# A hybrid encoder layer: weighing spread over two tiles, banks emptied during a pass's last tile, sparse sums added by VectorE, one normalization for both token tiles

## The chip, the cores and the metric

The kernel runs on one core of a Trainium2 chip. The metric is the device time of one execution in microseconds (us). TensorE (PE) multiplies, VectorE (DVE) and ScalarE (ACT) work on elements, GpSimd (POOL) issues the indirect DMAs, and SyncE (SP) issues the loads of weights. ACT issues DMAs too; each engine takes its instructions, DMAs among them, in order.

## The reference

One layer over 272 tokens of width 2048 (16 learned ones in front, 256 of the input): two mixers, a projection and a normalization, then a product-key expert layer, a second normalization, and the 256 input tokens as output. Only the expert layer and what follows matter here:

```python
qh = (xb @ w_pq).reshape(P_BLOCK, P_HEADS, 2, P_QDIM // 2)
...
eidx = jnp.take_along_axis(cidx, pos, axis=-1).reshape(P_BLOCK, P_HEADS * P_TOPK)
g = jax.nn.softmax(top, axis=-1).reshape(P_BLOCK, P_HEADS * P_TOPK).astype(xb.dtype)
act = jax.nn.gelu(jnp.einsum('td,tkd->tk', xb, u_tab[eidx]))
return jnp.einsum('tk,tkd->td', g * act, v_tab[eidx])
...
h = layer_norm(ALPHA * h + peer_ffn(h, w_pq[l], sub_keys[l], u_tab[l], v_tab[l]), ln2_g[l], ln2_b[l])
```

Each token picks 128 of 16384 experts; u_tab and v_tab are 16384 x 2048 each.

## The kernel before

For 224 of the 256 tokens (NT) the expert layer is computed densely: all activations gelu(x . u) for all experts, times a mostly zero matrix of weights g, times v. For the other 32 tokens (NS) it is computed sparsely, from gathered rows.

**u pass.** Tile j holds 128 experts; it comes as two half tiles of 128 x 1024 (n counts half tiles). `begin` loads one more half tile (SP, `raw`, 4 buffers) and splits it into two parts: ACT casts it to `wh` (L134), DVE subtracts to get `wl` (L137), 4 buffers each. In steady work the split of a unit is issued three units ahead of its matmuls. `product` issues a wl matmul (L1114) and a wh matmul over both halves of the input (L1115), three matmuls at the head of a bank (L1110 to L1112). `activation` empties the bank of a tile (`gather_out`: ACT copies the low half, L1055, DVE adds, L1057) and ACT applies the Gelu: for tiles below HELD = 70 into `slots` in SBUF, for later ones into spill groups of four (`ya`, in the same three buffers as `wv`, L1073), which ACT stores to `ad` in DRAM (L1075).

**The weights g.** POOL scatters them, 256 indirect DMAs (L957), into `gd` in DRAM. The sparse tokens' rows come by 32 indirect loads of u_rows and 32 of v_tab (L1031), two buffers; DVE uses each (L1018 for u, L1025 for v). `sparse(rate)` spreads these: 0.33 credits twice a tile in u from tile 28 on, 0.14 twice a tile in the value passes; each whole credit issues one fetch or one use.

**Value passes.** v is taken in two passes h = 0, 1 of 128 tiles, each tile 128 experts x 1024 columns, 8 column blocks d; bank `pv[d]` sums over the 128 tiles. The moving operand is made by `weigh(i)` for a pair of tiles: DVE multiplies the activations by the weights (L1094; in pass 1 only for the tiles that are loaded again, the others keep their product), ACT copies to `wv` (L1097), DVE subtracts (L1099). In even tiles its steps are issued after d = 0, 3 and 6, for the pair two further on. At the end of it ACT issues the next loads: weights (L1085), and for tiles from `far` = 108 on activations into one of two `ring` buffers (L1087). Tiles 70 to 107 come back in five bulk loads into `late[0]` (tile `over`, L1228). Pairs 0 and 1 are weighed at the last two half tiles of u.

**Between the passes** all eight banks are emptied after the last tile into `tmp` and stored to `fd` by ACT (L1247). **At the end** the last tile's banks are emptied behind each d, `turn_back(c, t)` turns 512 columns of a token tile t back with TensorE (L1262; for t = 1 also a `comb` matmul that adds the four parts of the sparse sums, L1261), DVE adds the residual (L1264) and takes statistics (L217); `ln2_finish(t)` normalizes each token tile by itself with DVE (L1279, L1283, L1285), ACT (L1276, L1281) and POOL (L1277, L1284).

PE, DVE, ACT and SP keep the order in which the program issues instructions; POOL's order is set by the scheduler.

Of the kernel before, what the change touches and what calls it, by code (L numbers as in the profile page):

```python
# [40 lines left out]
HELD, LATE = 70, 38  # L41
# [6 lines left out]
def hybrid_layer(ctx: ExitStack, tc: tile.TileContext, a: dict):  # L48
# [824 lines left out]
    gts = [home(2 * NT).rearrange("p (j t) -> p j t", t=NT) for _ in range(2)]  # L873
# [6 lines left out]
    ring = [mem[:, picks + 2 * NT * i:picks + 2 * NT * (i + 1)].rearrange("p (j t) -> p j t", t=NT) for i in range(2)]  # L880
# [199 lines left out]
    def fetch_weights(i):  # L1080

        h, m = divmod(i, P // 2)
        j = 2 * m
# [132 lines left out]
    later.append((P + 80, comb, a["c_comb"]))  # L1216
    for t in range(2):
        later.append((P + 81 + 2 * t, res[:, 4 * t:4 * t + 4, :NT], fd[4 * t:4 * t + 4].rearrange("d p t -> p d t")))
    for i in range(2):
        later.append((P + 88 + 8 * i, row2[i], a["ln_rows"][4 + i:5 + i, :].broadcast_to([P, D])))  # L1220
    stage = None
    for h in range(2):
        pv = [psum() for _ in range(8)]
        for j in range(P):
# [28 lines left out]
    st2 = [sm.tile([P, 4, 6], F32, name="bnst") for _ in range(2)]

    def turn_back(c, t):
        cs = slice(c * 512, (c + 1) * 512)
        ps = psum()
        for q in range(4):
            if t:

                nc.tensor.matmul(ps[:, q * P:(q + 1) * P], comb[:U], xsp[:U, c * 512 + q * P:c * 512 + (q + 1) * P], start=True, stop=False)  # L1261
            nc.tensor.matmul(ps[:, q * P:(q + 1) * P], res[:, 4 * c + q, t * P:(t + 1) * P], ident, start=t == 0, stop=True)  # L1262
        dst = fin[:, t, cs]
        nc.vector.scalar_tensor_tensor(out=dst, in0=dst, scalar=ALPHA, in1=ps, op0=ALU.mult, op1=ALU.add)  # L1264
# [111 lines left out]
```

## Time and profile before

| | |
|---|---|
| median of 3 runs | 1963.23 us (1961.41 to 1966.65) |
| the profiled execution | 1960.09 us, span 1958.3 us |
| busy: PE, weight load, DVE, ACT, POOL | 96%, 90%, 72%, 50%, 34% of the span |
| mean granted TensorE clock | 0.982 |
| u pass, about | 590 to 1239 us |
| value passes, about | 1243 to 1589 and 1591 to 1931 us |

A busy time is the sum over an engine's instructions; a granted clock of 1.00 is 2.4 GHz, 0.50 is 1.2 GHz. "idle before <- X" is the time for which the engine had nothing to do ahead of that instruction, and what ended it.

### The profile page before, as it was taken

The page shows a single profiled execution, that of the slowest core. Times are in us where ns is not written, and L with a number is a line of the kernel's source. Part 1 is how long each engine was busy: PE and PEld are TensorE (multiplying, and loading weights), DVE is VectorE, ACT ScalarE, POOL GpSimd, SP SyncE. Part 2 cuts the span into 40 slices and gives each one's busy share as a digit, 9 for nine tenths or more (in the row PEclk, how much of TensorE's full clock was granted, in tenths as well). Part 3 has the DMA queues.
Part 4 walks back from the last instruction along what each step waited for, and adds up shares of the span by engine and source line. Part 5 has one row for each costly group of instructions (what it writes and reads, how often), then busy time and mean ns, then how long its engine had stood idle before and what let it go on. Part 6 is the DMA issues. An engine that isn't in the chain of part 4 may idle for free.

```text
span 1958.3 us, 32249 instructions
## 1 busy us (share of the span) xinstructions
PE 1873.9 (96%) x12376; PEld 1761.0 (90%) x12376; DVE 1418.1 (72%) x2163; ACT 977.0 (50%) x1458; POOL 668.2 (34%) x381
## 2 busy tenths in 40 slices
PE   7999999998999999999999999899999879999995
PEld 5998998887999999899999999899999879999995
DVE  7674586656878999976767667677887667776767
ACT  5553554534446565455555545444554445555542
POOL 4000004001388883787877877010001011110002
PEclk9999998999999999999999999899999989999998
DMA  6974444364667787899999999799888867779882
GB/s 209 329 269 166 169 146 146 132 216 159 204 174 203 196 247 229 253 277 297 288 290 293 309 296 321 273 338 334 308 316 307 299 233 273 264 259 327 295 266 74
DMA packets 183293, 488.80 MB, mean 250 GB/s; under 512 B 52553, under 2 KB 83537, under 8 KB 173137
## 3 DMA queue, kind: packets, MB, share of 16 engines
q1 hardware_dynamic: 115312, 371.61, 55.6%
q0 software_dynamic: 47712, 76.41, 15.0%
q10 hardware_dynamic: 20112, 38.71, 5.5%
q8 instruction: 97, 1.59, 0.3%
q14 instruction: 60, 0.48, 0.1%
HBM read 458.92 MB, written 26.59 MB: 248 GB/s over the span
## 4 chain that ended last, share of the span: by engine, by line
PE 49%; DVE 10%; DMA 6%; issue 4%; ACT 4%; ACTq 0%; POOL 0%; DVEq 0%
PE ps L1115 29%; PE ps L1114 15%; DVE wl L137 4%; DMA raw<-v_tab 3%; ACT wh L134 2%; DMA raw<-u_tab 2%; PE ps L181 1%; PE ps L180 1%; PE ps L179 1%; DVE mem L1025 1%; DVE mem L1094 1%; DVE wv L1099 1%; PE ps L1112 1%; PE ps L1111 1%; ACT wv L1097 1%
## 5 line engine op out<-in xcount | busy, mean ns | idle before, releaser
L137 DVE TENSOR_TENSOR wl<-raw,wh 128x1024 fp32r<-128x1024 f32 x660 | 804.0, 1230 | 393.5 <-ACT wh L134 372.0
L134 ACT CAST wh<-raw 128x1024 fp32r<-128x1024 f32 x666 | 692.5, 1049 | 668.4 <-PE ps L1115 204.9
L1115 PE MATMUL ps<-wv,wh 128*128 128x448 f32 x2032 | 643.2, 376 | 0.0
L1115 PE MATMUL ps<-actT,wh 128*128 128x448 f32 x1920 | 603.7, 370 | 0.0
L1114 PE MATMUL ps<-wv,wl 128*128 128x224 f32 x2032 | 541.9, 267 | 12.2 <-DVE wl L137 12.1
L1114 PE MATMUL ps<-actT,wl 128*128 128x224 f32 x1920 | 511.1, 266 | 5.3 <-DVE wl L137 4.4
L957 POOL DMA_INDIRECT gd<-mem x256 | 486.9, 1902 | 83.4 <-issue 74.7
L1115 PEld LDWEIGHTS ps<-wv,wh 128*128 128x128 f32 x2032 | 383.9, 189 | 29.0
L1114 PEld LDWEIGHTS ps<-wv,wl 128*128 128x128 f32 x2032 | 390.5, 192 | 18.0 <-DVE wl L137 17.9
L1115 PEld LDWEIGHTS ps<-actT,wh 128*128 128x128 f32 x1920 | 359.8, 187 | 20.9
L1114 PEld LDWEIGHTS ps<-actT,wl 128*128 128x128 f32 x1920 | 365.4, 190 | 7.8 <-DVE wl L137 6.7
L179 PE MATMUL ps<-actT,wh 128*128 128x256 f32 (+1 forms) x944 | 277.4, 294 | 4.9 <-ACT actT L350 4.9
L180 PE MATMUL ps<-actT,wh 128*128 128x256 f32 (+1 forms) x944 | 271.9, 288 | 4.4 <-POOL actT L229 4.2
L181 PE MATMUL ps<-actT,wl 128*128 128x256 f32 (+1 forms) x944 | 270.7, 287 | 0.0
L1031 POOL DMA_INDIRECT mem<-v_tab,mem x32 | 56.0, 1749 | 532.2 <-DVE mem L1025 477.2
L179 PEld LDWEIGHTS ps<-actT,wh 128*128 128x128 f32 x944 | 181.4, 192 | 12.6 <-ACT actT L350 5.1
L180 PEld LDWEIGHTS ps<-actT,wh 128*128 128x128 f32 x944 | 181.4, 192 | 7.1 <-POOL actT L229 5.8
L181 PEld LDWEIGHTS ps<-actT,wl 128*128 128x128 f32 x944 | 181.1, 192 | 0.0
L1097 ACT CAST wv<-mem 128x448 fp32r<-128x448 f32 x90 | 50.8, 564 | 123.7 <-DVE mem L1094 121.1
L1099 DVE TENSOR_TENSOR wv<-mem,wv 128x448 fp32r<-128x448 f32 x90 | 56.1, 623 | 31.0 <-ACT wv L1097 31.0
L1031 POOL DMA_INDIRECT mem<-u_rows,mem x32 | 50.5, 1577 | 71.0 <-DVE mem L1018 57.6
L1018 DVE CUSTOM_DVE_ANT_0 mem<-mem 128x2048 f32<-128x2048 f32 x32 | 73.1, 2285 | 0.0
(281 smaller groups left out, 1652.5 us busy)
## 6 DMA issues: line engine op xcount, KB each, us to landing
raw<-u_tab SPq DMA_DIRECT2D x256, 512.0 KB
raw<-v_tab SPq DMA_DIRECT2D x256, 512.0 KB
raw<-w_in SPq DMA_DIRECT2D x86, 512.0 KB
mem<-gd ACTq DMA_DIRECT2D x74, 224.0 KB
raw<-w_out SPq DMA_DIRECT2D x32, 512.0 KB
raw<-w_pq SPq DMA_DIRECT2D x32, 512.0 KB
gd<-mem SPq DMA_DIRECT2D x16, 896.0 KB
ad<-ya ACTq DMA_DIRECT2D x14, 448.0 KB
```

The lines of the kernel that those rows point to most:

```text
L134: acts.append(order(nc.scalar.copy(out=wh, in_=raw)))
L137: subs.append(order(nc.vector.tensor_tensor(out=wl, in0=raw, in1=wh.bitcast(F32), op=ALU.subtract)))
L179: nc.tensor.matmul(out, wh, ah, start=first, stop=False)
L180: nc.tensor.matmul(out, wh, al, start=False, stop=False)
L181: nc.tensor.matmul(out, wl, ah, start=False, stop=last)
L957: s = nc.gpsimd.indirect_dma_start(out=gdf[:, :], out_offset=bass.IndirectOffsetOnAxis(ap=idx, axis=0), in_=val, in_offset=None, compute_o ...
L1018: nc.vector.tensor_tensor_reduce(out=buf[:U], in0=buf[:U], in1=xsp[:U], scale=1.0, scalar=0.0, op0=ALU.mult, op1=ALU.add, accum_out=sact[: ...
L1031: f = nc.gpsimd.indirect_dma_start(out=buf[:U], out_offset=None, in_=a["u_rows" if n < K else "v_tab"], in_offset=bass.IndirectOffsetOnAxi ...
L1097: nc.scalar.copy(out=w[:, :, 0], in_=x)
L1099: nc.vector.tensor_tensor(out=w[:, :, 1], in0=x, in1=w[:, :, 0].bitcast(F32), op=ALU.subtract)
L1114: nc.tensor.matmul(lo, wl, x[:, 0], start=False, stop=False)
L1115: nc.tensor.matmul(two(ps)[:, :, :NT], wh, x, start=False, stop=last)
```

## The change

`weigh` becomes four steps: the mult after d = 0 of an even tile; copy and load of weights after d = 0 of the odd one; the subtraction after its d = 5; the load of activations after d = 3 of the next even tile. Loads run three pairs ahead, in three buffers each, and HELD falls from 70 to 68 to make room. The first three weight loads stand 12 half tiles before the end of u instead of 2, pair 0 is weighed 4 half tiles before the end, pair 1 after the last activation. The sparse rate in u is 0.34, and 0 in the last two tiles. The banks of pass 0 are emptied behind each d of its last tile, into other buffers (`spare`), with no sparse step there. The sparse sums are added in pass 1: POOL copies three 32-row parts of `xsp` to `over` at tile 110, and DVE adds the four parts into `fin` at tiles 114, 116, 118 and 120. `ln2_finish` runs once: one chain for both tiles, ACT scales tile 1, DVE does the rest, and POOL nothing.

```diff
-HELD, LATE = 70, 38
+HELD, LATE = 68, 38
...
-        if i < P and (h == 0 or j >= far):
-            nc.scalar.dma_start(out=gts[m % 2], in_=gd[:, j:j + 2])
+        if i < P and (h == 0 or 2 * m >= far):
+            nc.scalar.dma_start(out=gts[i % 3], in_=gd[:, 2 * m:2 * m + 2])
+    def fetch_activations(i):
+        j = 2 * (i % (P // 2))
         if i < P and j >= far:
-            nc.scalar.dma_start(out=ring[m % 2], in_=ad[:, j - HELD:j - HELD + 2])
+            nc.scalar.dma_start(out=ring[i % 3], in_=ad[:, j - HELD:j - HELD + 2])
...
         if h == 0 or j >= far:
-            nc.vector.tensor_tensor(out=x, in0=x, in1=gts[m % 2], op=ALU.mult)
-            yield
+            nc.vector.tensor_tensor(out=x, in0=x, in1=gts[i % 3], op=ALU.mult)
+        yield
         w = g.tile([P, 2, 2, NT], F32R, name="wv", bufs=3)
         nc.scalar.copy(out=w[:, :, 0], in_=x)
+        fetch_weights(i + 3)
         yield
         nc.vector.tensor_tensor(out=w[:, :, 1], in0=x, in1=w[:, :, 0].bitcast(F32), op=ALU.subtract)
         wv[i] = w
-        fetch_weights(i + 2)
+        yield
+        fetch_activations(i + 3)
...
-        if n == 2 * P - 2:
+        if n == 2 * P - 12:
             scatter_some(len(scatters))
-            fetch_weights(0)
-            fetch_weights(1)
+            for m in range(3):
+                fetch_weights(m)
...
-                    sparse(0.33 if j >= 28 else 0)
+                    sparse(0.34 if 28 <= j < P - 2 else 0)
...
-        if n == 2 * P - 2:
+        if n == 2 * P - 4:
             whole_of(weigh(0))
-        if n == 2 * P - 1:
-            whole_of(weigh(1))
...
     whole_of(activation(P - 1, ps))
+    whole_of(weigh(1))
...
+            if h == 1 and j == 110:
...
+                for i in range(G - 1):
+                    nc.gpsimd.dma_start(out=others[i][ND:], in_=xsp[i * NS:(i + 1) * NS])
+            if h == 1 and j >= 114 and j % 2 == 0 and joined[0] < G:
...
+                    nc.vector.scalar_tensor_tensor(out=own, in0=own, scalar=ALPHA, in1=xsp[ND:], op0=ALU.mult, op1=ALU.add)
...
+                    nc.vector.tensor_tensor(out=own, in0=own, in1=others[i - 1][ND:], op=ALU.add)
...
-                if j % 2 == 0 and d in (0, 3, 6) and stage:
-                    next(stage, None)
-                if d == 4:
+                if d == 0 or (d == 5 and j % 2):
+                    next(now, None)
+                if d == 3 and j % 2 == 0 and before:
+                    next(before, None)
+                if d == 4 and not (h == 0 and j == P - 1):
                     sparse(0.14)
-        if h == 0:
-            for d in range(8):
-                y = tmp()[:, :NT]
-                whole_of(gather_out(two(pv[d]), y))
-                nc.scalar.dma_start(out=fd[d], in_=y)
+                if h == 0 and j == P - 1:
+                    y = spare(d)
+                    whole_of(gather_out(two(pv[d]), y))
+                    nc.scalar.dma_start(out=fd[d], in_=y)
...
+    def ln2_finish():
+        nm = sm.tile([P, 2], F32, name="nb")
+        rsqrt_eps(mv2[:, 1], mv2[:, 1], 1.0)
...
+            nc.scalar.activation(out=fin[:, 1, cs], in_=fin[:, 1, cs], func=AF.Identity, scale=mv2[:, 1, 1:2], bias=nm[:, 1:2])
...
+            nc.vector.scalar_tensor_tensor(out=y, in0=y, scalar=mv2[:, 0, 0:1], in1=row2[0][:, cs], op0=ALU.subtract, op1=ALU.mult)
+            nc.vector.scalar_tensor_tensor(out=y, in0=y, scalar=mv2[:, 1, 0:1], in1=row2[1][:, cs], op0=ALU.mult, op1=ALU.add)
...
+            nc.vector.tensor_tensor(out=y, in0=y, in1=row2[0][:, cs], op=ALU.mult)
+            nc.vector.tensor_tensor(out=y, in0=y, in1=row2[1][:, cs], op=ALU.add)
```

The order that this makes is seen at three places. First DVE near the end of pass 0, before (`mem<-mem` and `over` of 128x448 are the mult, `wv` the subtraction, L1025 a sparse row):

```order
L1099 TENSOR_TENSOR wv<-mem,wv 128x2x224
L137 TENSOR_TENSOR wl<-raw,wh 128x1024 x2
L1094 TENSOR_TENSOR mem<-mem 128x448
L1025 SCALAR_TENSOR_TENSOR mem<-mem 128x2048
L1099 TENSOR_TENSOR wv<-mem,wv 128x2x224
```

and changed:

```order
L1104 TENSOR_TENSOR wv<-mem,wv 128x2x224
L137 TENSOR_TENSOR wl<-raw,wh 128x1024
L1098 TENSOR_TENSOR mem<-mem 128x448
L1025 SCALAR_TENSOR_TENSOR mem<-mem 128x2048
L137 TENSOR_TENSOR wl<-raw,wh 128x1024
L1104 TENSOR_TENSOR wv<-mem,wv 128x2x224
```

A wl, for which DVE waits for a cast of ACT and not for the copy, now stands between the mult and the subtraction of a pair. Second ACT from the first load of weights to the copy of pair 2, before:

```order
L1085 DMA mem<-gd 128x448 x2
L1055 COPY tmp<-ps 128x224
L1073 ACTIVATE ya<-tmp 128x224
L1075 DMA ad<-ya 128x896
L1097 CAST wv<-mem 128x2x224
L1085 DMA mem<-gd 128x448
L134 CAST wh<-raw 128x1024
L1097 CAST wv<-mem 128x2x224
L1085 DMA mem<-gd 128x448
L1073 ACTIVATE ya<-tmp 128x224
L1055 COPY tmp<-ps 128x224
L1073 ACTIVATE ya<-tmp 128x224
```

and changed, from the copy of pair 0 on:

```order
L1101 CAST wv<-mem 128x2x224
L1084 DMA mem<-gd 128x448
L134 CAST wh<-raw 128x1024 x2
L1055 COPY tmp<-ps 128x224
L1073 ACTIVATE ya<-tmp 128x224
L134 CAST wh<-raw 128x1024
L1073 ACTIVATE ya<-tmp 128x224
L1055 COPY tmp<-ps 128x224
L1073 ACTIVATE ya<-tmp 128x224
L1075 DMA ad<-ya 128x896
L1101 CAST wv<-mem 128x2x224
L1084 DMA mem<-gd 128x448
```

The copies of pairs 0 and 1 no longer stand ahead of the last two Gelus; pair 0's comes ahead of three casts, pair 1's behind the last store. Third DVE in pass 1 about tile 116, changed (L1250 and L1252 are the sparse additions; before there is no such instruction):

```order
L1250 SCALAR_TENSOR_TENSOR mem<-mem 32x2048
L1098 TENSOR_TENSOR mem<-mem 128x448
L137 TENSOR_TENSOR wl<-raw,wh 128x1024
L1104 TENSOR_TENSOR wv<-mem,wv 128x2x224
L137 TENSOR_TENSOR wl<-raw,wh 128x1024
L1252 TENSOR_TENSOR mem<-mem,over 32x2048
```

One addition stands in front of the mult of each of four pairs.

## Rows read from the trace of the kernel before

**Rows 1.** Busy time by stretch: start:end, length, PE, PEld, DVE, ACT, POOL, PEclk, DMA share, GB/s

```profile
1239.45:1255.09 15.64, 8.69 (x39) 7.81 (x39) 7.91 (x11) 6.24 (x12) 0.37 (x1) 0.67 0.72 248
1255.09:1588.70 333.61, 322.50 (x2019) 303.13 (x2017) 259.57 (x269) 159.51 (x191) 30.74 (x18) 0.99 0.88 312
1588.70:1606.64 17.94, 10.45 (x37) 8.42 (x37) 7.44 (x13) 4.88 (x10) 2.38 (x1) 0.62 0.59 202
1606.64:1922.57 315.93, 314.79 (x2006) 299.70 (x2005) 217.87 (x209) 157.20 (x184) 20.68 (x13) 1.00 0.78 272
1922.57:1958.30 35.73, 13.82 (x113) 13.22 (x111) 28.83 (x56) 8.23 (x16) 9.89 (x6) 0.76 0.16 60
```

**Rows 2.** Timeline, u to v: start, duration, engine, line, out<-in, [idle before <- releaser]

```profile
1240.39 0.33 ACTq L1075 DMA_DIRECT2D ad<-ya  x1
...
1242.64 0.37 PE L1110 MATMUL ps<-wv,wh 128*128 128x224 f32 x1 [3.04 <-ACT wv L1097]
...
1249.16 0.39 ACT L1073 ACTIVATE ya<-tmp 128x224 f32<-128x224 f32 x1 [3.23 <-DMA ad<-ya]
...
1255.09 0.26 PE L1114 MATMUL ps<-wv,wl 128*128 128x224 f32 x1
```

**Rows 3.** Waits of PE in 1255.09 to 1588.7: total us, times, longest

```profile
PE ps L1114 <- DVE wl L137: 10.9, 12, 1.9
```

**Rows 4.** Timeline of DVE and ACT at the end of pass 0

```profile
1525.15 0.62 DVE L1094 TENSOR_TENSOR mem<-mem 128x448 f32<-128x448 f32 x1
...
1525.80 0.57 ACT L1097 CAST wv<-mem 128x448 fp32r<-128x448 f32 x1 [4.01 <-DVE mem L1094]
...
1526.40 0.63 DVE L1099 TENSOR_TENSOR wv<-mem,wv 128x448 fp32r<-128x448 f32 x1 [0.63 <-ACT wv L1097]
...
1527.48 1.99 ACT L134 CAST wh<-raw 128x1024 fp32r<-128x1024 f32 x2 [1.11 <-DVE wv L1099]
1528.56 2.36 DVE L137 TENSOR_TENSOR wl<-raw,wh 128x1024 fp32r<-128x1024 f32 x2 [1.53 <-ACT wh L134]
...
1530.83 0.62 DVE L1094 TENSOR_TENSOR mem<-mem 128x448 f32<-128x448 f32 x1
```

**Rows 5.** Timeline between the passes

```profile
1590.18 0.39 DVE L1057 TENSOR_TENSOR tmp<-ps,tmp 128x224 f32<-128x224 f32 x1
...
1594.02 0.39 DVE L1057 TENSOR_TENSOR tmp<-ps,tmp 128x224 f32<-128x224 f32 x1 [0.83 <-ACT tmp L1055]
...
1596.79 0.35 ACT L1055 COPY tmp<-ps 128x224 f32<-128x224 f32 x1 [2.81 <-DMA fd<-tmp]
...
1603.16 0.41 PE L1114 MATMUL ps<-wv,wl 128*128 128x224 f32 x1
```

**Rows 6.** Line 1025, the sparse rows of v: ns min/median/max, first and last start

```profile
L1025 DVE SCALAR_TENSOR_TENSOR mem<-mem x31: 2344/2347/2348, 1280.3 to 1838.1; 128x2048 f32<-128x2048 f32 x31
```

**Rows 7.** Busy time of a stretch with bulk loads (columns of rows 1)

```profile
1320.00:1330.00 10.00, 8.67 (x55) 8.03 (x54) 8.09 (x11) 4.58 (x6) 1.08 (x1) 1.00 1.00 347
```

**Rows 8.** Timeline of POOL, the last scatter

```profile
1218.93 1.55 POOL L957 DMA_INDIRECT gd<-mem  x1 [0.30 <-issue]
```

**Rows 9.** Timeline of the tail

```profile
1937.14 1.41 DVE L1279 SCALAR_TENSOR_TENSOR mem<-mem,bnmv 128x512 f32<-128x512 f32 x2
...
1938.07 3.27 POOL L1277 TENSOR_TENSOR mem<-mem 128x512 f32<-128x512 f32 x2 [123.01 <-ACT mem L1276]
1938.46 3.42 DVE L1283 SCALAR_TENSOR_TENSOR mem<-mem,bnmv 128x512 f32<-128x512 f32 x2
...
1943.48 0.68 DVE L1264 SCALAR_TENSOR_TENSOR mem<-mem,ps 128x512 f32<-128x512 f32 x1
...
1953.18 1.43 DVE L1285 TENSOR_TENSOR mem<-mem 128x512 f32<-128x512 f32 x1 [0.24 <-ACT mem L1281]
```

**Rows 10.** Line 1134, multiplications and additions on 512: ns min/median/max

```profile
L1134 DVE TENSOR_TENSOR mem<-mem x16: 673/682/1214, 485.2 to 527.2; 128x512 f32<-128x512 f32 x16
```

More of the change, by code (lines that the diff above doesn't have):

```diff
@@ L872, in hybrid_layer @@
     gb = [home(D) for _ in range(2)]
-    gts = [home(2 * NT).rearrange("p (j t) -> p j t", t=NT) for _ in range(2)]
+    gts = [home(2 * NT).rearrange("p (j t) -> p j t", t=NT) for _ in range(3)]
     picks = keep[0]
@@ L879, in hybrid_layer @@
     eidx = home(P).bitcast(U32)
-    ring = [mem[:, picks + 2 * NT * i:picks + 2 * NT * (i + 1)].rearrange("p (j t) -> p j t", t=NT) for i in range(2)]
+    ring = [mem[:, picks + 2 * NT * i:picks + 2 * NT * (i + 1)].rearrange("p (j t) -> p j t", t=NT) for i in range(3)]
     spick, sg, sact, sw = (home(K) for _ in range(4))
@@ L1208, in hybrid_layer @@
     row2 = [mem[:, D * i:D * (i + 1)] for i in (2, 3)]
-    res = mem[:, 4 * D:4 * D + KT * S].rearrange("p (d t) -> p d t", t=S)
-    comb = mem[:, 6 * D:6 * D + P]
+    res = mem[:, 4 * D:4 * D + KT * NT].rearrange("p (d t) -> p d t", t=NT)
+    others = [over[:, D * i:D * (i + 1)] for i in range(G - 1)]
     later = deque()
@@ L1215, in hybrid_layer, with spare @@
         later.append((P + 64 + 8 * t, fin[:, t], hd[t]))
-    later.append((P + 80, comb, a["c_comb"]))
     for t in range(2):
-        later.append((P + 81 + 2 * t, res[:, 4 * t:4 * t + 4, :NT], fd[4 * t:4 * t + 4].rearrange("d p t -> p d t")))
+        later.append((P + 81 + 2 * t, res[:, 4 * t:4 * t + 4], fd[4 * t:4 * t + 4].rearrange("d p t -> p d t")))
     for i in range(2):
         later.append((P + 88 + 8 * i, row2[i], a["ln_rows"][4 + i:5 + i, :].broadcast_to([P, D])))
-    stage = None
+    now = before = None
+    joined = [0]
+    def spare(d):
+        return sm.tile([P, L], F32, name="out", tag=("acc", "work", "acc", "work", "pT", "pT")[d % 6])[:, :NT]
     for h in range(2):
@@ L1228, in hybrid_layer @@
                 nc.scalar.dma_start(out=dst, in_=src)
-            if h == 1 and j == 80:
-                nc.gpsimd.memset(res[:, :, NT:], 0.0)
+            if h == 1 and j == 110:
+                while flight or issued[0] < 2 * K:
+                    sparse(1)
+                for i in range(G - 1):
+                    nc.gpsimd.dma_start(out=others[i][ND:], in_=xsp[i * NS:(i + 1) * NS])
+            if h == 1 and j >= 114 and j % 2 == 0 and joined[0] < G:
+                i = joined[0]
+                joined[0] += 1
+                own = fin[ND:, 1]
+                if i == 0:
+                    nc.vector.scalar_tensor_tensor(out=own, in0=own, scalar=ALPHA, in1=xsp[ND:], op0=ALU.mult, op1=ALU.add)
+                else:
+                    nc.vector.tensor_tensor(out=own, in0=own, in1=others[i - 1][ND:], op=ALU.add)
             if h == 1 and j == P - 1:
@@ L1248, in hybrid_layer @@
+                if d == 3 and j % 2 == 0 and before:
+                    next(before, None)
+                if d == 4 and not (h == 0 and j == P - 1):
+                    sparse(0.14)
+                if h == 0 and j == P - 1:
+                    y = spare(d)
+                    whole_of(gather_out(two(pv[d]), y))
+                    nc.scalar.dma_start(out=fd[d], in_=y)
     assert not later
-    while flight or issued[0] < 2 * K:
-        sparse(1)
+    assert joined[0] == G
     st2 = [sm.tile([P, 4, 6], F32, name="bnst") for _ in range(2)]
+    mv2 = sm.tile([P, 2, 2], F32, name="bnmv2", bufs=1)
@@ L1255, in turn_back @@
     def turn_back(c, t):
         cs = slice(c * 512, (c + 1) * 512)
+        n = P if t == 0 else ND
         ps = psum()
         for q in range(4):
[L1259 to L1264, printed above, removed]
@@ L1290, in hybrid_layer @@
+    turns = deque((c, t) for c in range(4) for t in range(2))
     w = got.popleft()
@@ L1292, in hybrid_layer @@
         value(pv, *w, P - 1, d, 1)
-        whole_of(gather_out(two(pv[d]), res[:, 8 + d, :NT]))
-        if d >= 2 and turns:
+        whole_of(gather_out(two(pv[d]), res[:, 8 + d]))
+        for _ in range(1 if 2 <= d < 7 else 0):
             turn_back(*turns.popleft())
-    for t in range(2):
-        for c in (2, 3):
-            turn_back(c, t)
-        ln2_finish(t)
+    while turns:
+        turn_back(*turns.popleft())
+    ln2_finish()
     whole.__exit__(None, None, None)
```

46 lines of the change are left out of this document (18 added, 28 removed).

## The prediction

> **What bounds the kernel now.** Read first the busy time stage by stage [rows 1]. TensorE sets the pace: in the long stretch of the second value pass it is busy 314.79 of 315.93 us, for 1002 pairs of matmuls (the wl and the wh one of a column block), so a pair takes 0.314 us, a tile of eight 2.51 us and a pass of 1024 pairs 322 us. The same work takes much longer elsewhere, and only that excess can be won. One execution is the base: 1960.09 us, its span 1958.3; the median of the runs is 1963.23, 3.1 us (0.16%) higher, and the sum is carried over to it unchanged. About 0.3% (5.9 us) is what a measurement of this kernel can tell from no change.
>
> Four places hold the excess. (1) **u to v**, 1239.45 to 1255.09: 15 pairs are begun in 15.64 us instead of some 4.8, at a granted clock of 0.67 [rows 1]; 10.8 us too long. TensorE first waits 3.04 us for the weighing of pair 0 (ACT wv); then ACT's queue stands 3.23 us before a Gelu that needs the buffer of a store issued at 1240.39, so that the last u bank leaves late [rows 2]. (2) **The first value pass**, 1255.09 to 1588.70: 1009 pairs need 317.0 us and take 333.61; 16.6 us too long, 10.9 of it in 12 waits for DVE's wl [rows 3], the rest the restart behind each and a dip of the clock. (3) **First to second pass**: the last tile begins at 1588.70 - 2.51 = 1586.2, and the first tile of the second pass ends at 1603.16, 17.0 us on instead of 5.1. The first sum leaves a bank at 1590.18, the fourth at 1594.02 (1.28 us apart), then ACT waits 2.81 us for a store to fd to free a buffer [rows 5]. (4) **The tail**, 1922.57 to the end, 35.73 us, in which DVE is busy 28.83 [rows 1].
>
> Why DVE is late in place 2 is seen in its instructions [rows 4]: mult (0.62), then ACT's copy which had waited 4.01 us for it, then the subtraction, which waits for the copy, then ACT's two casts, which had to wait for the subtraction (a load of activations stands between them in ACT's queue and needs it), then two wl, then the next mult: 5.68 us from mult to mult, where TensorE needs 5.03 for two tiles. A sparse row of 2.35 us [rows 6] comes on top. The ring is closed, so its period counts, not DVE's busy time, which is 0.62 + 0.63 + 2.36 = 3.61 us a pair.
>
> **The change part by part.**
>
> *Weighing.* The mult is issued at the even tile, the copy at the odd, the subtraction late in the odd one, and the ring's load half a pair on. ACT then finds the mult done, and no instruction of the loop waits for one issued just ahead of it. What is left on DVE is 3.61 us a pair and, at 0.14 rows a tile, 0.28 x 2.35 = 0.66: 4.3 of 5.03 us. A wl is ready some 2.4 us after its tile's turn (cast 1.0, wl 1.2 [rows 4]) and is needed three tiles (7.5 us) on, so a sparse row, even with a wl ahead of it, fits into the slack of 5.1. I take 2 us for what remains in the first pass, since the bulk loads of spilled tiles fill the DMA for a while: in 1320 to 1330 its share is 1.00, and TensorE is busy 8.67 of 10 us [rows 7]. Bounds: 0, and all 16.6 (rival A). Gain 14.6 us. The same ring paces the end of pass two, where TensorE loses 1.1 us of 315.93 [rows 1]: gain 1.0.
>
> *u to v.* Pair 0 is weighed two half tiles earlier, and the sparse rows pause for the last two u tiles; both lie beside TensorE's u work, which has the 5.1 us of slack. With 68 held tiles the last spill group is full (124 to 127), so no Gelu needs another buffer. Late next: the copy of pair 2 needs the buffer of that group, whose store is issued some 1.4 us after the last u matmul. The store of before was issued at 1240.39 and had landed by 1249.16 at the latest [rows 2], 8.8 us; with that, copy and subtraction are through 11.4 us after u, and pair 2 is due after 4 tiles, 10.1. I take a stall of 0.8 us, as ACT may have resumed behind the landing; bounds 0 and 3. Gain 10.8 - 0.8 = 10.0. The Trainium skill (DMA: Bandwidth & Descriptors, Anatomy of one DMA) gives a transfer some 2.0 us and its bytes over 436 GB/s, by which I estimate 3.1 us for these 448 KB: then nothing stalls and the sum would be 0.8 us better; the row, on a busy DMA, says otherwise, and the sum goes by it.
>
> *The first weights* are now loaded 12 half tiles before the end of u, about 1239.45 - 6 x 5.03 = 1209.3, by ACT, which must wait there until the last scatter has landed. Queued behind are the casts of u: the next but one must have its wl by 1219.4, so ACT may stand until about 1217. In the kernel before the last scatter starts at 1218.93 and takes 1.55 us [rows 8], and POOL waits for nothing ahead of it; with 0.34 instead of 0.33 the last row's use comes three tiles earlier (15 us, of which POOL's lag eats some 5) but eight scatters stand behind it instead of five (6 us): last end near 1216, landed near 1218. Price 1.0 us; bounds 0 and 6 (rival C).
>
> *Banks.* The gathers of the last tile stand behind each d, but ACT could read bank 0 then already; what changes is that DVE has no sparse row there, so the first sum ends about 2.8 us into the tile (cast, copy of wv, copy of the bank, add) instead of 4.4, and that six spare buffers take the sums, so nothing waits for fd. The store stays in ACT's queue, so the spacing stays 1.28: the eighth bank leaves after 2.8 + 7 x 1.28 + 0.2 = 12.0, the tile ends 0.8 later, 12.8 instead of 17.0. Gain 4.2; bounds 2 and 8 (spacing 1.5, or 0.7, the copy and the issue alone). The clock falls here as before (0.62), so that is in both.
>
> *Sparse sums.* Sixteen comb matmul instructions a turn become eight, beside DVE's work: nothing. Instead DVE takes four additions over 2048 elements in tiles 114 to 120. No row shows one over 32 partitions; the nearest is the sparse row over 128, 2.35 us [rows 6]. A pair of tiles then costs DVE 3.61 + 2.35 = 5.96 of 5.03 us, so it falls 3.7 us behind in four pairs, against 5.1 of slack. Nothing; bounds 0 and 3. POOL's three copies start six tiles ahead, with nothing behind them; its memset goes.
>
> *Tail.* Before, from 1943.48 to the end of the last DVE instruction at 1954.61 stand two turns (2 x 1.37) and one whole finish, 8.4 us; there are two, 16.8. Within each, two instructions take 0.71 apiece, but the next two of the same shape 1.71, and a tensor addition 1.43, all while POOL multiplies [rows 9]; alone, such a multiplication or addition of 512 takes 0.68 [rows 10]. After: one chain of small instructions for both tiles (15 instead of 11, so 2.7 us for 2.0), 8 x 0.71 and 8 x 0.68, with ACT's four beside them: 13.8. Gain 3.0 us, if POOL's absence makes DVE fast; if those times are the instructions' own, 4 x 1.0 and 8 x 0.75 come on top and 7.0 is lost (rival B).
>
> **Sum**: 14.6 + 1.0 + 10.0 - 1.0 + 4.2 + 3.0 = 31.8 us. The execution would take 1928.3, the median **1931.4 us**.
>
> **The rivals.**
> A, *the ring does not open*: DVE, 86% busy, falls behind often enough that ACT's copy still waits for the mult and the casts behind it come late; pass one keeps its 16.6 us. For it: 4.3 of 5.03 us leaves little to catch up with. Against: pass two runs with the same wl and rows at full speed. Gain 31.8 - 14.6 = 17.2, so 1946.0 us. Chance 17%.
> B, *slow instructions*: the 1.43 and 1.71 us are the instructions' own. Against: the pair of 0.71 has the same shape. The tail loses 7.0 instead of winning 3.0: 1941.4 us. Chance 8%. The Trainium skill (Perfetto Trace Analysis, Optimizing Scalar/DVE Operations) advises to offload from a saturated VectorE to ScalarE or even GpSimd, which speaks against taking POOL's share back; it adds that the two share a read port and that it might not help. By the first half the result is this rival, and the slow rows with POOL at work speak for the second.
> C, *early load*: POOL ends as late as before, at 1220.5 and the landing behind it, so ACT stands to 1222 or 1223 and TensorE loses 6 us instead of 1: 1936.4 us. Chance 9%.
> D, *slower*: DMA becomes the bound in the value passes, since three sets of weights instead of two are in flight. In pass one it moved 312 GB/s [rows 1], 1.65 MB a pair of tiles. At that rate for good a pair takes 5.29 us, as now. It decides from where the rate falls below about 297: then the other gains (17.2 us over 63 pairs, 0.27 each) are gone. At 280 a pair takes 5.89, 38 us more over 63 pairs, and the time is 1946.0 + 38 = 1984 us. Against: with a share of 1.00 it moved 347 [rows 7], and the share of pass one is 0.88 [rows 1]. Chance 4%.
>
> **How the numbers follow.** 62% for the forecast, 17, 8, 9 and 4% for A to D. The forecast's own bounds, not all at one end at once, give 1922 to 1938; the range goes on to A and just past it, 1921 to 1948. A and C or B together, with the tail of A, leave some 3% within 5.9 us of before; D is slower, 4%; faster is 93%.
>
> **What would show it.** Right: between the u pass and the first value pass no wait of over 1 us but one at tile 4; in pass one less than 3 us of waits for wl and no ACT wait of 4 us for a mult; bank sums 1.3 us apart without a wait for fd; a DVE tail without an instruction of over 0.8 us on 512 elements, some 32.6 us from the last tile to the end. Wrong: pass one above 330 us, a hole near tile 122 of u, or TensorE waiting in tiles 114 to 126 of pass two.

## The result, and the profile after

The changed kernel takes 1932.64 us (median of 5 runs, 1929.15 to 1937.37), the kernel before 1963.23 (5 runs beside it): a ratio of 0.9846, 95% interval 0.9826 to 0.9866, so 26 to 34 us faster. 1931.4 had been forecast. Measured again beside the kernel before (e12, the last experiment) the ratio was 0.987 (0.9848 to 0.9892). The profiled execution of the changed kernel took 1929.15 us with a span of 1927.3; against the span of before, 1958.3, that is 31.0 us less. The sum had said 31.8, but its terms came out differently, and two misses were covered by other things.

The stretches that answer to [rows 1], in the columns of [rows 1] (u to v, first value pass, join, second pass, tail):

```profile
1239.60:1255.00 15.40, 15.08 (x102) 14.16 (x101) 12.79 (x16) 9.39 (x14) 0.94 (x1) 1.00 0.86 301
1255.00:1569.58 314.58, 309.66 (x1957) 294.07 (x1956) 248.20 (x263) 159.53 (x186) 31.42 (x17) 0.99 0.92 327
1569.58:1581.00 11.42, 8.26 (x33) 6.52 (x33) 4.92 (x11) 4.88 (x10) 0.00 (x0) 0.70 0.66 230
1581.00:1895.80 314.80, 314.80 (x2011) 300.48 (x2011) 228.62 (x215) 157.51 (x184) 17.54 (x15) 1.00 0.80 277
1895.80:1927.30 31.50, 7.59 (x49) 5.93 (x47) 26.15 (x55) 5.63 (x12) 0.00 (x0) 0.65 0.18 67
```

After u nothing stops: in 15.4 us TensorE starts 47 pairs of matmuls at a granted clock of 1.00, where it had started 15 in 15.64. The first pass needs 307 us for its 978.5 pairs and takes 314.6, so 7.5 are still lost, of 16.6. The second pass loses nothing, the four additions of VectorE included. The waits of the first pass (total us, times, longest), which answer to [rows 3]:

```profile
PE ps L1121 <- DVE wv L1104: 4.9, 3, 2.4
ACT wh L134 <- DMA raw<-v_tab: 88.7, 63, 4.0
ACT wv L1101 <- DVE mem L1098: 18.5, 23, 2.7
ACT wv L1101 <- DVE over L1098: 12.0, 11, 2.5
```

The same waits of ACT in the kernel before, 1255 to 1588.7 (the waits for the mult of a spilled tile, `over`, were 45.6 us more):

```profile
ACT wv L1097 <- DVE mem L1094: 95.8, 41, 4.3
ACT wh L134 <- DMA raw<-v_tab: 14.7, 15, 2.9
```

TensorE no longer waits for wl. ACT's waits for a mult have fallen from 141.4 to 30.5 us; it now arrives early enough to wait for the raw tiles of v instead, 88.7 us. Nearly all of that costs TensorE nothing. Where it does, the new stall is this (timeline, columns of [rows 2]):

```profile
1318.75 1.05 ACT L134 CAST wh<-raw 128x1024 fp32r<-128x1024 f32 x1 [2.42 <-DMA raw<-v_tab]
1319.70 0.56 ACT L1101 CAST wv<-mem 128x448 fp32r<-128x448 f32 x1
...
1319.83 1.23 DVE L137 TENSOR_TENSOR wl<-raw,wh 128x1024 fp32r<-128x1024 f32 x1 [1.70 <-ACT wh L134]
1320.97 2.35 DVE L1025 SCALAR_TENSOR_TENSOR mem<-mem 128x2048 f32<-128x2048 f32 x1
1323.23 0.62 DVE L1104 TENSOR_TENSOR wv<-mem,wv 128x448 fp32r<-128x448 f32 x1
...
1323.91 0.47 PE L1121 MATMUL ps<-wv,wh 128*128 128x448 f32 x1 [2.36 <-DVE wv L1104]
```

A raw tile comes late, so its cast and its wl come late. In DVE's order a sparse row of 2.35 us stands between that wl and the subtraction of the pair (block 4 before block 5 of the odd tile), so the subtraction starts only at 1323.23. The copy is not what holds it: it was done by 1320.26. The other two waits (0.74 us to 1506.97, 1.77 us to 1544.41) have the same order of late cast, wl, row and subtraction. Behind the longest one the granted clock fell, to 0.50 in 1325 to 1327 and 0.65 in the next 2 us, which is about 2 us of the other 2.6 of the 7.5; behind the two shorter ones it stayed at 1.00.

At tile 122 of u is the hole that rival C named. ACT's loads of the first weights wait for GpSimd's scatters:

```profile
1206.09 1.05 ACT L134 CAST wh<-raw 128x1024 fp32r<-128x1024 f32 x1 [1.36 <-PE ps L1121]
1213.76 1.51 ACTq L1084 DMA_DIRECT2D mem<-gd  x3
1215.32 0.34 ACT L1055 COPY tmp<-ps 128x224 f32<-128x224 f32 x1 [8.18 <-issue]
...
1210.12 1.55 POOL L957 DMA_INDIRECT gd<-mem  x1 [0.30 <-issue]
...
1215.85 1.98 ACT L134 CAST wh<-raw 128x1024 fp32r<-128x1024 f32 x2
1216.94 0.37 PE L1116 MATMUL ps<-actT,wh 128*128 128x224 f32 x1 [0.91 <-ACT wh L134]
1218.19 0.37 PE L1118 MATMUL ps<-actT,wl 128*128 128x224 f32 x1 [0.78 <-DVE wl L137]
```

ACT stands 8.18 us, then TensorE waits for the next cast and its wl, 1.7 us together, and the granted clock is 0.55 to 0.60 from 1219 to 1223. u takes 653.2 us instead of 649.5.

At the other places, [rows 2], [rows 5] and [rows 9] are answered by these (u to v; banks; tail):

```profile
1242.87 0.33 ACTq L1075 DMA_DIRECT2D ad<-ya  x1
1249.35 0.56 ACT L1101 CAST wv<-mem 128x448 fp32r<-128x448 f32 x1 [3.62 <-DMA ad<-ya]
...
1569.81 0.33 ACTq L1270 DMA_DIRECT2D fd<-out  x1
1570.98 0.33 ACTq L1270 DMA_DIRECT2D fd<-out  x1
...
1578.90 0.41 PE L1120 MATMUL ps<-wv,wl 128*128 128x224 f32 x1
...
1912.70 0.75 DVE L1300 SCALAR_TENSOR_TENSOR mem<-mem,bnmv 128x512 f32<-128x512 f32 x1
1913.49 0.75 DVE L1301 SCALAR_TENSOR_TENSOR mem<-mem,bnmv 128x512 f32<-128x512 f32 x1
...
1923.21 0.69 DVE L1307 TENSOR_TENSOR mem<-mem 128x512 f32<-128x512 f32 x1
```

The copy of pair 2 waits for the store, as forecast, but only to 1249.35, and TensorE doesn't notice. The stores of the banks follow 1.17 us apart without a wait. In the tail no VectorE instruction on 512 elements takes over 0.8 us.

### The profile page after: what moved, and what is told of

The parts are those of the page before. It is cut to its first block, busy times and chain, and to the rows that moved or that the text cites. A ratio compares the mean times of both kernels' runs of the same rounds, so it can differ in the third digit from the quotient of the medians.

```text
span 1927.3 us, 32115 instructions
## 1 busy us (share of the span) xinstructions
PE 1856.5 (96%) x12312; PEld 1748.3 (91%) x12312; DVE 1422.0 (74%) x2167; ACT 979.3 (51%) x1454; POOL 660.3 (34%) x377
## 4 chain that ended last, share of the span: by engine, by line
PE 43%; DVE 12%; DMA 11%; issue 4%; ACT 2%; POOL 2%; ACTq 0%; DVEq 0%; POOLq 0%
PE ps L1121 25%; PE ps L1120 12%; DMA raw<-v_tab 7%; DVE wl L137 5%; DMA raw<-u_tab 2%; ACT wh L134 2%; POOL gd L957 1%; PE ps L181 1%; PE ps L180 1%; PE ps L179 1%; DVE wv L1104 1%; DVE mem L1025 1%; DMA gd<-mem 1%; DVE mem L1098 1%; DMA raw<-w_pq 1%
## 5 line engine op out<-in xcount | busy, mean ns | idle before, releaser
L957 POOL DMA_INDIRECT gd<-mem x256 | 495.9, 1937 | 83.4 <-issue 75.3
L1031 POOL DMA_INDIRECT mem<-v_tab,mem x32 | 50.3, 1571 | 524.6 <-DVE mem L1025 489.1
L1025 DVE SCALAR_TENSOR_TENSOR mem<-mem 128x2048 f32<-128x2048 f32 x31 | 72.7, 2345 | 0.0
```

The lines of the kernel that those rows point to most:

```text
L957: s = nc.gpsimd.indirect_dma_start(out=gdf[:, :], out_offset=bass.IndirectOffsetOnAxis(ap=idx, axis=0), in_=val, in_offset=None, compute_o ...
L1025: nc.vector.scalar_tensor_tensor(out=xsp[:U], in0=buf[:U], scalar=sw[:U, k:k + 1], in1=xsp[:U], op0=ALU.mult, op1=ALU.add)
L1031: f = nc.gpsimd.indirect_dma_start(out=buf[:U], out_offset=None, in_=a["u_rows" if n < K else "v_tab"], in_offset=bass.IndirectOffsetOnAxi ...
```

## The experiments

Times of different chips are compared through the ratio to the kernel before, run beside each. For the stages I use one profiled execution each; the boundaries are first and last starts of two lines (here the changed kernel: the first matmul of a bank, and the wh matmul of a pair):

```profile
L1116 PE MATMUL ps<-actT,wh x128: 262/263/370, 586.2 to 1234.7; 128*128 128x224 f32 x128
L1116 PE MATMUL ps<-wv,wh x16: 262/370/556, 1239.7 to 1578.1; 128*128 128x224 f32 x16
L1121 PE MATMUL ps<-wv,wh x2032: 371/375/602, 1243.0 to 1900.7; 128*128 128x448 f32 x185
L1121 PE MATMUL ps<-actT,wh x1920: 368/371/602, 586.6 to 1239.4; 128*128 128x448 f32 x192
```

u is 586.2 to 1239.4; the gap, to 1239.7; pass 0, to its last matmul (1569.3, timeline); the join, to 1578.1; pass 1, to 1900.7; the rest to 1927.3.

| execution | u starts | u | gap | pass 0 | join | pass 1 | end | span |
|---|---|---|---|---|---|---|---|---|
| before | 589.7 | 649.5 | 3.4 | 345.8 | 14.0 | 328.3 | 27.6 | 1958.3 |
| changed | 586.2 | 653.2 | 0.3 | 329.6 | 8.8 | 322.6 | 26.6 | 1927.3 |
| e12, changed again | 586.1 | 653.8 | 0.2 | 331.7 | 8.9 | 322.6 | 26.6 | 1929.9 |
| e1, old weighing | 588.0 | 652.8 | 0.2 | 351.4 | 9.8 | 334.2 | 26.6 | 1963.0 |
| e9, order alone | 586.5 | 651.4 | 8.3 | 326.9 | 14.9 | 327.9 | 27.6 | 1943.5 |
| e5, late weighing | 590.9 | 654.8 | 3.0 | 331.1 | 10.9 | 322.8 | 26.6 | 1940.1 |
| e6, banks at the end | 592.1 | 653.9 | 0.2 | 329.8 | 13.6 | 323.6 | 26.6 | 1939.8 |
| e7, GpSimd in tail | 589.9 | 653.2 | 0.2 | 334.1 | 8.8 | 322.9 | 27.8 | 1936.9 |
| e2, load later | 586.1 | 655.4 | 0.2 | 335.4 | 9.7 | 324.1 | 26.6 | 1937.5 |
| e3, row after sub | 587.4 | 659.8 | 0.2 | 329.3 | 11.4 | 323.2 | 26.6 | 1937.9 |
| e4, both | 587.6 | 651.5 | 0.2 | 337.1 | 11.3 | 323.6 | 26.6 | 1937.9 |
| e10, GpSimd loads | 589.7 | 649.0 | 0.2 | 325.4 | 8.9 | 322.6 | 26.2 | 1922.0 |
| e11, loads spread | 594.7 | 648.6 | 0.2 | 334.4 | 8.9 | 323.8 | 26.5 | 1937.1 |

Two columns warn against reading single executions too finely: u starts anywhere from 586.1 to 594.7, ahead of what the edits touch, and pass 0 of kernels with the new order scatters from 325 to 337.

**Is it the order of the weighing? e1_old_weighing and e9_order_alone.** The first keeps all of the change but the order; the second puts the order alone, with two buffers, into the kernel before.

```diff
 e1, in the changed kernel
-                if d == 0 or (d == 5 and j % 2):
-                    next(now, None)
-                if d == 3 and j % 2 == 0 and before:
-                    next(before, None)
+                if j % 2 == 0 and d in (0, 3, 6):
+                    next(now, None)
 (both loads behind the subtraction, for pair i + 3)
 e9, in the kernel before: these lines the other way round
 (weights for pair i + 2 behind the copy, activations one step after the subtraction)
```

> The changed kernel with its three sets of weights and three ring buffers kept, but the weighing issued as before: mult, copy and subtraction at blocks 0, 3 and 6 of the even tile, both loads behind the subtraction. Theory (the order opens the ring): ACT's copy waits some 4 us for the mult again, the casts stand behind it, the first value pass has some 10 us of waits for wl and takes 338 to 340 us where the changed kernel took 330; the time is 8 to 10 us above the changed kernel's 1932.6, some 1941 to 1943. Rival (the third buffers open it, since a load then finds its buffer free for a whole pair longer): the copy's wait may return but no cast comes late, and the time stays within 2 us of 1932.6. Second rival (the 8 us that the first value pass still loses are the DMA's and are lost in any order): below 1938.

Measured: 1966.75 us, 1.0015 of before (1.0001 to 1.0028). All of the gain is gone, over three times what the theory said.

```profile
1241.00:1592.77 351.77, 332.15 (x2057) 309.44 (x2055) 266.84 (x279) 164.66 (x200) 26.86 (x18) 0.99 0.88 307
...
PE ps L1119 <- DVE wl L137: 19.1, 25, 1.9
ACT wv L1101 <- DVE mem L1098: 100.9, 43, 4.3
```

That is its first pass: the wait of ACT for the mult is back, and 19.1 us of waits for wl with it. Its u to v is as short as in the changed kernel (gap 0.2), yet from the end of u to the end of pass 0 it takes 351.6 us, and the kernel before 349.2. The ring paces the pass from its first mult on: 63 pairs from 1237.7 to 1580.8, 5.45 us a pair (before 5.36, changed 5.12). So what e1 wins ahead of the pass it loses in it. Part of the loss is that its period is 0.09 us longer than that of before, 5.7 us over 63 pairs; why is not shown. Pass 1 is 334.2 instead of 322.6 us (before: 328.3), with 8.2 us of waits for wl from 1888 on that the changed kernel doesn't have there. The theory of the order held; its size, and with it the adding up of terms, did not.

> The kernel before with the new order of the weighing alone: mult at the even tile, copy in the odd one, subtraction late in it, ring load half a pair on; two buffers, 70 held tiles and all else as before. Theory (the order opens the ring): ACT's copy waits no more for the mult, the waits for wl in the first value pass fall from 10.9 to under 5 us, and the time is 9 to 15 us below that of before, 1949 to 1955. Rival one (a third buffer is needed, as a load is now issued half a pair later and finds too little time with two): waits for wl or for mult stay, less than 4 us gained. Rival two (the experiment that undid the order cost all 34 us, so order and the other parts only pay together): within 3 us of 1964.

Measured: 1946.13 us, 0.9906 (0.9883 to 0.9928), 14 to 23 us gained, at or above the theory's 9 to 15. Two buffers suffice; both rivals fell. In 1238 to 1573 the waits were

```profile
PE ps L1117 <- ACT wv L1102: 7.9, 1, 7.9
PE ps L1122 <- DVE wv L1105: 1.8, 3, 0.7
ACT wv L1102 <- DVE mem L1099: 35.2, 30, 5.0
```

7.9 us before the first pair (3.0 in the kernel before, where the loads of the weights start at the same place: with u's last half tiles), and then next to nothing. So the order alone is worth some 18 us, the other parts some 12 with it and none without it.

**u to v: e5_late_weighing.**

```diff
-        if n == 2 * P - 4:
+        if n == 2 * P - 2:
             whole_of(weigh(0))
+        if n == 2 * P - 1:
+            whole_of(weigh(1))
```

> The changed kernel with pair 0 weighed in the second-last and pair 1 in the last half tile of u, as before the change; 68 held tiles and three buffers stay. Theory (half of the gain from u to v is the weighing of pair 0 being early, half the spill group that no longer makes a Gelu wait): TensorE waits 2 to 3 us for ACT's copy of pair 0 and runs some 5 us at the lower clock, 4 to 6 us in all, 1937 to 1939. Rival (what is lost ahead of the first value pass is given back in it, since casts and wl then have a lead when the bulk loads come): the wait is there, but the time stays within 2 us of 1932.6.

Measured: 1934.34 us, 0.9827 (0.9805 to 0.985): not slower than the changed kernel. TensorE did wait 2.7 us for the copy of pair 0, so the wait belongs to the late weighing, and the rival's time came out. That pass 0 gives it back isn't shown: it took 331.1 us, as in e12. The 3 us are less than these runs can separate (1928.80 to 1941.90).

**Banks: e6_banks_at_the_end.**

```diff
-                if h == 0 and j == P - 1:
-                    y = spare(d)
-                    whole_of(gather_out(two(pv[d]), y))
-                    nc.scalar.dma_start(out=fd[d], in_=y)
+        if h == 0:
+            for d in range(8):
+                y = tmp()[:, :NT]
+                whole_of(gather_out(two(pv[d]), y))
+                nc.scalar.dma_start(out=fd[d], in_=y)
```

(and the sparse row is let into that tile again)

> The changed kernel with the banks of the first value pass emptied after its last tile, through the shared temporary buffers, and with the sparse row in that tile, as before the change. Theory (banks leave earlier and find free buffers): the first sum leaves 4.0 to 4.5 us instead of 2.3 us after the last tile began, ACT waits 2 to 3 us for a store, and the first tile of the second pass ends 17 instead of 11.8 us after the last tile began: 5 us more, 1937 to 1939. Rival (only the buffers count, as ACT could read the banks that early before): 2 to 3 us more.

Measured: 1938.3 us, 0.9859 (0.9836 to 0.9883); the interval overlaps the changed kernel's, so the time alone decides nothing. The join does: 13.6 us instead of 8.8.

```profile
1580.66 0.33 ACTq L1271 DMA_DIRECT2D fd<-tmp  x1
1585.08 0.35 ACT L1055 COPY tmp<-ps 128x224 f32<-128x224 f32 x1 [4.87 <-DMA fd<-tmp]
1585.88 0.33 ACTq L1271 DMA_DIRECT2D fd<-tmp  x1
```

The wait for a store to free a buffer makes 4.0 of the 4.8 us (ACT is idle 4.87 us where it is 0.82 to 0.90 between other sums); issuing the gathers early makes about half a microsecond: the first bank is waited for 0.73 us there, 0.19 in the changed kernel. The size was the theory's, the reason mostly the rival's. No sparse row fell into that tile in e6 (the last one ran from 1566.40), so what the missing row is worth, a first sum 2.8 us into the tile instead of 4.4, is not tested.

**Tail: e7_pool_in_tail.**

```diff
-            nc.vector.tensor_tensor(out=y, in0=y, in1=row2[0][:, cs], op=ALU.mult)
+            eng = nc.gpsimd if c == 3 else nc.vector
+            eng.tensor_tensor(out=y, in0=y, in1=row2[0][:, cs], op=ALU.mult)
 (and the addition alike)
```

> The changed kernel with the last 512 columns of token tile 1 multiplied and added by GpSimd. Theory (VectorE's 1.43 and 1.71 us of before come from GpSimd working beside it): the VectorE instructions that run in the some 6.5 us of GpSimd's two take 1.4 to 1.7 us instead of 0.69 to 0.75, about four of them, 3.6 us more less 1.4 us for the two handed over: the end of the tail is 1 to 3 us later. Rival (those durations were the instructions' own): all stay at 0.69 to 0.75 and the end comes up to 1 us earlier.

Measured: 1937.42 us, 0.9857 (0.9825 to 0.9888), open by itself. From the last pair to the end 27.8 us instead of 26.6, and

```profile
1924.01 0.75 DVE L1300 SCALAR_TENSOR_TENSOR mem<-mem,bnmv 128x512 f32<-128x512 f32 x1
1924.25 1.63 POOL L1307 TENSOR_TENSOR mem<-mem 128x512 f32<-128x512 f32 x1 [99.27 <-ACT mem L1296]
1924.79 1.63 DVE L1301 SCALAR_TENSOR_TENSOR mem<-mem,bnmv 128x512 f32<-128x512 f32 x1
1925.95 1.59 POOL L1308 TENSOR_TENSOR mem<-mem 128x512 f32<-128x512 f32 x1
1926.35 1.75 DVE L1300 SCALAR_TENSOR_TENSOR mem<-mem,bnmv 128x512 f32<-128x512 f32 x1
1928.12 0.75 DVE L1301 SCALAR_TENSOR_TENSOR mem<-mem,bnmv 128x512 f32<-128x512 f32 x1
```

The two VectorE instructions beside GpSimd's take 1.63 and 1.75 us, those before and after 0.75. Rival B fell. Two were slowed and not four, since each of GpSimd's took 1.6 us; the 3.27 us of [rows 9] are two of them. The Trainium skill (Perfetto Trace Analysis, Optimizing Scalar/DVE Operations) says that a saturated VectorE may be offloaded even to GpSimd, and that this might not help, as the two share a read port. The rows agree with the warning: 1.63 and 1.75 us instead of 0.75.

**What is still lost: e2_load_later, e3_row_after_sub, e4_both.**

```diff
 e2
         if n == 2 * P - 12:
             scatter_some(len(scatters))
+        if n == 2 * P - 8:
             for m in range(3):
                 fetch_weights(m)
 e3
-                if d == 4 and not (h == 0 and j == P - 1):
+                if d == 6 and not (h == 0 and j == P - 1):
```

> The changed kernel with its first three loads of weights issued 8 instead of 12 half tiles before the end of u, the remaining scatters handed over where they were. Theory (ACT stands at tile 122 of u until the last scatter has landed, near 1213.8, and the casts and bank copies behind it come late): TensorE's 1.7 us of waits at 1216.9 and 1218.2 and the dip of the clock behind them go, 3 to 4 us less, some 1929. Rival (the hole at tile 122 is the loads of u that come late behind the scatters' traffic, whatever ACT does): the waits stay and the time is within 1 us of 1932.6. Second rival (the loads now come too late for the weighing of pair 0): a wait of 1 to 3 us at the first value tile, no gain.

Measured: 1929.56 us, 0.9819 (0.9803 to 0.9836). The stand at tile 122 only moved: in the profiled execution GpSimd was late (its last scatter from 1223.14 to 1225.30, the one before 3.52 us long), ACT stood 6.4 us until 1227.65, TensorE waited 1.5 us for wh and 0.8 for wl, and u took 655.4. In e4, with the same edit, ACT hardly stood (0.5 us). So a later load doesn't remove the stand; whether it makes it rarer, two executions don't show. The time is better than the theory's bound asks, but its interval overlaps the changed kernel's.

> The changed kernel with the sparse rows of the value passes at block 6 of a tile instead of block 4, so behind the subtraction of an odd tile and not ahead of it. Theory (the three stalls of the first value pass, 4.9 us, are a subtraction that stands behind a row of 2.35 us in DVE's queue when wh came late): those waits fall below 1 us and with the clock dips behind them 4 to 7 us go, 1926 to 1929. Rival (the DMA, with raw tiles late, is the cause and the row only the last in the queue): the waits move to wl or to the next mult and the time falls by less than 2 us.

Measured: 1939.46 us, 0.987 (0.9853 to 0.9886): no gain shown. No wait for a subtraction was left, but 3.2 us in seven waits for wl, and pass 0 took 329.3 us as without the edit (329.6). That fits the rival: late raw tiles are the cause, the row only the last in the queue. With pass 0 between 325 and 337 us from one execution to the next, a gain of a few us would not be seen. The same execution showed how far the hole at tile 122 can go:

```profile
1217.48 1.55 POOL L957 DMA_INDIRECT gd<-mem  x1 [0.31 <-issue]
...
1220.55 1.54 ACTq L1084 DMA_DIRECT2D mem<-gd  x3
1222.13 0.35 ACT L1055 COPY tmp<-ps 128x224 f32<-128x224 f32 x1 [15.05 <-issue]
```

ACT stood 15 us instead of 8, with four more scatters left, TensorE waited 7.8 us for wh, and u took 659.8 us. The edit acts only later, in the value passes, so this is not its doing.

> Both edits together: first weights 8 half tiles before the end of u, sparse rows behind the subtraction. If both theories hold the gains add up, 7 to 10 us below the changed kernel, 1923 to 1926; if only one holds, that one's time; if the waits move elsewhere, within 2 us of 1932.6.

Measured: 1929.11 us, 0.9827 (0.9807 to 0.9847); the gains don't add. Its execution shows a second thing that varies: the seventh sum takes the first one's buffer and waits for its store, 9.1 us after that was issued.

```profile
1576.94 0.33 ACTq L1271 DMA_DIRECT2D fd<-out  x1
...
1586.04 0.39 DVE L1057 TENSOR_TENSOR out<-ps,tmp 128x224 f32<-128x224 f32 x1 [3.29 <-DMA fd<-out]
```

The wait was absent in the executions of changed, e12, e1 and e7, and 1.7, 3.3, 3.3 and 2.9 us in e2 to e5.

**Both removed: e10_pool_load, e11_spread_loads, e12_changed_again.**

```diff
 e10
             for m in range(3):
-                fetch_weights(m)
+                nc.gpsimd.dma_start(out=gts[m], in_=gd[:, 2 * m:2 * m + 2])
-                    y = spare(d)
+                    y = spare(d) if d < 6 else tmp()[:, :NT]
 e11 = e10 and
-    for lo in range(0, LATE, 8):
-        later.append((16 + lo // 2, ..., lo:min(lo + 8, LATE)
+    for lo in range(0, LATE, 4):
+        later.append((6 + 2 * lo, ..., lo:min(lo + 4, LATE)
```

> The changed kernel with the first three loads of weights issued by GpSimd, straight behind its own last scatter, and with eight buffers for the sums of the first value pass instead of six (the last two take temporary ones). Theory (two costs that differ from execution to execution remain: ACT standing 8 to 15 us at tile 122 of u until the last scatter has landed, and the seventh bank's sum waiting 0 to 3.3 us for the store of the first to fd): from the first to the last matmul of u 650 to 652 us instead of 653 to 660, no DVE wait for fd, and the median 3 to 6 us below the unchanged copy on the same chip. Rival (the late casts of u come from the scatters' traffic): u stays at 653 or more, the gain is under 2 us.

> As the run before, and the spilled activations come in ten loads of 4 tiles at every eighth tile from 6 to 78 instead of five of 8 tiles at every fourth from 16 to 32. Theory (what the first value pass still loses, some 8 us with waits for wl and the subtraction, are raw tiles late behind the bulk loads, when DMA moves 340 to 410 GB/s): the loss between 1290 and 1350 goes, 2 to 4 us less than the run before. Rival one (the losses near 1500 to 1560, where the rows and the ring's loads fill the DMA, are the larger part and stay): under 2 us. Rival two (the bulk only moves): no gain, waits spread over the pass.

> The changed kernel itself again, for comparison on the same chip. Both theories: 0.983 to 0.986 of before, some 1930 to 1935 us; the profiled execution again differs from the first one in the stand of ACT at tile 122 and in the wait of the seventh bank by a few us.

Measured on one chip: e10 1927.1 us, 0.982 (0.9798 to 0.9841); e11 1929.08, 0.9825 (0.9806 to 0.9843); e12 1935.19, 0.987 (0.9848 to 0.9892). e10 is faster than both kernels: 34.7 us below before, 8 below the changed one, with intervals apart. GpSimd does the waiting, where no cast stands behind it, and u takes 649.0 us (653.8 in e12):

```profile
1211.10 1.80 POOL L957 DMA_INDIRECT gd<-mem  x1 [0.30 <-issue]
1216.57 1.75 POOL L1191 DMA_DIRECT2D mem<-gd  x3 [3.67 <-DMA gd<-mem]
```

The longer list of buffers, the second edit of e10, is not tested by this: neither e10 nor e12 waited for fd in its execution. Spreading the bulk loads gives nothing: in e11 TensorE waited 7.1 us for the subtraction, in six places from 1280 to 1565, 2.0 us of it near 1425 where the changed kernel has no bulk load (its last is issued at 1326.03). Rival two. What sets pass 0 apart between executions, 325 to 337 us, stays open. ACT's waits for raw tiles, 66 to 102 us in every execution with the new order (15 and 18 in before and e1), are seen in all; a remedy was not found. The rate of 0.34, the sums on VectorE and the 68 held tiles were not undone one by one.

## Why the prediction was right

By terms, from the profiled executions (the pass 0 term is 16.6 less 7.5; the others from the stretches above, the join from the last tile's start, 1566.97, to 1578.90, the tail from 1895.74):

| term | forecast | found |
|---|---|---|
| weighing, pass 0 | 14.6 | 9.1 |
| end of u to first value pass | 10.0 | 10.2 |
| banks | 4.2 | 5.1 |
| tail | 3.0 | 4.2 |
| weighing, pass 1 | 1.0 | 2.6 |
| early weights | -1.0 | -3.7 |
| start of u, not in the sum | 0 | 3.5 |
| sum | 31.8 | 31.0 |

*Weighing.* The mechanism was right: ACT's waits for the mult fell to about a fifth (141.4 to 30.5 us, the longest 4.3 to 2.7), wl is no longer waited for, and e1 and e9 show the order to be the cause. "ACT then finds the mult done" is too strong: ACT still waited for it in 34 places, 0.9 us each on average. The term that was mis-sized is "I take 2 us for what remains": 7.5 us remained. The slack of 5.1 us was reckoned from a wl ready 2.4 us after its tile's turn, so from a raw tile that is there by then. But ACT, set free, runs into the raw tiles (88.7 us of waits for 14.7), and behind a late wl the row stands ahead of the subtraction.

*Adding up.* The sum took each place's excess as won by itself. That was harmless for the forecast, since the ring opened, but it makes rival A's price wrong: it kept 17.2 us for the other parts and gave 1946.0, and e1, its mechanism, measured 1966.75 beside 1964.53. Had the ring stayed closed, the time would have been outside the range.

*u to v.* Right in place and size. The stall of 0.8 us did not come: the store, issued at 1242.87, let ACT resume at 1249.35, 6.5 us on, where 8.8 had been taken. By the Trainium skill's rule (DMA: Bandwidth & Descriptors, Anatomy of one DMA), 2.0 us and the bytes at 436 GB/s, I had estimated 3.1. The page gives that rule for DMAs issued by GpSimd, and ScalarE issued this one; the 6.5 us measured are twice the estimate.

*Early weights.* Mis-sized: 3.7 us instead of 1.0. The scatters were not later than forecast, though some took up to 2.5 us and not 1.55: tile 122 began at 1205.89 in this execution (1209.3 in the forecast), and the loads went out 7.9 us behind that, where 8.7 had been reckoned (1218). What the price left out is what stands behind the wait: ACT issues three loads (1.51 us) and empties a bank before the cast at 1215.85, so TensorE waited 1.7 us, and the clock fell behind it. It is a draw at each execution: ACT stood 8.2 and 10.7 us in two executions of the changed kernel and 15 in e3, where the last scatter ended at 1219.03, near what rival C says, and u took 10.3 us more than before. So the bound of 6 us was too low as well.

*Banks.* Right in size; the spacing was 1.17 and not 1.28 us. By e6 some 4 us of it are the buffers'. That six buffers make "nothing wait for fd" holds in four of eight executions.

*Tail, sums.* Fast instructions without GpSimd, as forecast, 31.6 us from the last tile to the end where 32.6 was said. The additions of VectorE cost nothing beside an open ring; by e1 they are not free beside a closed one, though that run does not separate them from the ring itself.

*Weighing, pass 1.* The 2.6 us are not all the ring's: TensorE lost 1.1 us there before, and the rest was not taken apart.

*DMA bound* (rival D): not seen as such, 327 GB/s in pass 0 against 312; but late raw tiles stand at the head of each of the three waits that TensorE has left there.

Of the signs of being wrong one came, the hole near tile 122. The stretch of pass one took 314.6 us, and TensorE did not wait in tiles 114 to 126 of pass two.

So the mechanisms of the large terms were right, and that the time came out within 1.3 us is in part luck: 5.5 us too much for pass 0 and 2.7 too little for the early load met 0.9 to 1.6 us more at three other places and 3.5 us from ahead of u. Those 3.5 us belong to the execution and not to the change.

## What to carry to other kernels

Where an in-order engine waits for an instruction that another engine was handed just ahead, look for the loop that closes through both queues; its period is what counts, and time won in front of such a loop is not won until it is opened. Price parts together, or undo one in the finished kernel as well as adding it alone: here the order was worth 18 us alone and 33 as the last part. A load that must wait for a slow producer belongs on the queue of that producer, not on one with casts behind it.

## What was not expected of the hardware

- VectorE's instruction of 0.75 us took 1.63 and 1.75 us beside GpSimd's tensor operations (e7), and GpSimd's own 1.6 us there.
- A store of one 128x224 sum to memory took from under 6.6 us (no wait in the changed kernel) to 9.1 us (e4) from issue to the release of its buffer.
- GpSimd's indirect scatters took 1.55 us at the least and 1.83 in the median of 256 (changed kernel), but 2.0 to 3.5 us in some places of the same stretch (3.08 in e10, 3.52 in e2).
- The same program stood 8.2 us at tile 122 in one execution and 10.7 in another, though its last scatter ended earlier in the second (1210.05, 1211.67 in the first): ACT had come 1.9 us sooner, and its loads went out 4.1 us behind the scatter's end instead of 2.1.
- The start of u differs by 8.6 us between executions, 0.4% of the time, ahead of anything that was edited.
